# A tile of its own for every group of images, and all loads ahead of all stores on SP's ring, in a 180-degree rotation

## The chip, the cores and the metric

The kernel runs on one core of one Trainium2 chip; the other seven are idle. The metric is the device time of one execution in microseconds (us), as the median of several executions. A difference below 2% counts as "same", so nearly everything below is about why something large did not happen, and about effects of tenths of a per cent.

## The reference

```python
x = randn(32, 3, 256, 256).astype(float32)        # 25.17 MB
out = np.rot90(x, k=2, axes=(-2, -1))             # every 256x256 image turned by 180 degrees
```

Turning by 180 degrees is reversing the 65536 elements of each of the 96 images. There is no arithmetic: 25.17 MB come in, 25.17 MB go out.

## The kernel before: the parts that matter

The images are handled in three groups of 32. A group is a tile of 128 partitions by 16384 elements: four partitions for each image. The store's access pattern reverses the four quarters (`::-1`), VectorE reverses the elements within a partition.

```python
x4 = x.rearrange("b c h w -> (b c) (h w)").rearrange("(g n) (s e) -> g (n s) e", n=32, s=4)
o4 = out.rearrange("b c h w -> (b c) (h w)").rearrange("(g n) (s e) -> g n s e", n=32, s=4)
A  = pool.tile([P, E], ...)    # E = 16384: 64 KB a partition; Bt and Ct are the same
T  = pool.tile([P, J], ...)    # J = E // 8 = 2048

def load(t, g, lo=0, hi=E):
    nc.sync.dma_start(out=t[:, lo:hi], in_=x4[g][:, lo:hi])
def store(t, g):
    nc.sync.dma_start(out=o4[g][:, ::-1, :], in_=t[:, :])
# copy is a VectorE copy; back(t, lo, hi) is t[:, lo:hi] read backwards
def across(dst, src):                      # out of one tile into another: 4 copies
    for c in range(0, E, K):               # K = E // 4 = 4096
        copy(dst[:, c:c + K], back(src, E - c - K, E - c))
def inside(t):                             # in place, by way of T: 12 copies
    for lo in range(0, E // 2, J):
        hi = E - lo - J
        copy(T[:, :], back(t, hi, hi + J))
        copy(t[:, hi:hi + J], back(t, lo, lo + J))
        copy(t[:, lo:lo + J], T[:, :])

load(A, 0, 0, N); load(A, 0, N, E)         # N = 512
load(Bt, 1)
across(Ct, A);  store(Ct, 0)
load(A, 2)                                 # has to wait until A has been read out
inside(Bt);     store(Bt, 1)
across(Ct, A);  store(Ct, 2)
```

Below, "load 0" and "store 0" are those of group 0, and so on. Every DMA is issued from SP (the sync engine, which does nothing else here), so all of them are in one ring: the queue of one issuing engine, which the 16 DMA engines worked off in order. A "packet" is the piece that the profile records for one DMA engine, and a transfer "lands" when its last one is reported complete. ACT, below, is ScalarE, which issues into a ring of its own.

Of the kernel before, what the change touches and what calls it, by code (L numbers as in the profile page):

```python
# [2 lines left out]

os.environ.setdefault("NEURON_RT_ULTRASERVER_MODE", "4")

# [4 lines left out]


@with_exitstack
def kernel(
    ctx: ExitStack,
    tc: tile.TileContext,
    x: bass.AP,
    out: bass.AP,
):









    nc = tc.nc
    P = 128  # L30

    B, C, H, W = x.shape
    L = H * W
    G = 32
    E = L // 4
    K = E // 4
    J = E // 8
    N = E // 32

    x4 = x.rearrange("b c h w -> (b c) (h w)").rearrange(  # L40
        "(g n) (s e) -> g (n s) e", n=G, s=4)
    o4 = out.rearrange("b c h w -> (b c) (h w)").rearrange(
        "(g n) (s e) -> g n s e", n=G, s=4)

    pool = ctx.enter_context(tc.tile_pool(name="slots", bufs=1))
    A = pool.tile([P, E], x.dtype, tag="A")
    Bt = pool.tile([P, E], x.dtype, tag="B")
    Ct = pool.tile([P, E], x.dtype, tag="C")
    T = pool.tile([P, J], x.dtype, tag="T")

    def back(t, lo, hi):
        return t[:, hi - 1:(lo - 1 if lo else None):-1]

    def copy(dst, src):
        tc.keep_in_program_order(nc.vector.tensor_copy(out=dst, in_=src))  # L55

    def load(t, g, lo=0, hi=E):
        nc.sync.dma_start(out=t[:, lo:hi], in_=x4[g][:, lo:hi])  # L58

    def store(t, g):  # L60
        nc.sync.dma_start(out=o4[g][:, ::-1, :], in_=t[:, :])  # L61

    def across(dst, src):
        for c in range(0, E, K):
            copy(dst[:, c:c + K], back(src, E - c - K, E - c))

    def inside(t):
        for lo in range(0, E // 2, J):
            hi = E - lo - J
# [4 lines that stand above are left out]
    load(A, 0, 0, N)  # L74
    load(A, 0, N, E)
    load(Bt, 1)
    across(Ct, A)
    store(Ct, 0)
    load(A, 2)
    inside(Bt)  # L80
    store(Bt, 1)
    across(Ct, A)
    store(Ct, 2)


# [1 line left out]
_INS = ['x']  # L87
_OUTS = [((32, 3, 256, 256), 'float32')]


# [23 lines left out]
```

## Time and profile before

| | before |
|---|---|
| time, median of 3 | 123.36 us |
| span in the profile | 121.2 us |
| moved | 50.33 MB, mean 415 GB/s |
| share of the 16 DMA engines' span filled by packets | 97.4% |
| VectorE busy | 32.5 us, 20 copies |

A share of 97.4% says that the DMA engines are the bound. One more view, of SP's own waits, tells who holds back the issue of a transfer. Columns: who waited, for what, us in total, times, longest.

```profile
SPq L61 <- DVE Ct L55: 61.5, 2, 32.0
SPq L61 <- DVE Bt L55: 15.1, 1, 15.1
SPq L61 <- DMA Bt<-in_x_dram: 10.2, 1, 10.2
```

SP waits for VectorE in 76.6 of the 121.2 us (61.5 + 15.1).

### The profile page before, as it was taken

What the parts mean: (1) busy time and instruction counts of PE and PEld (TensorE: products, weight loads), DVE (VectorE), ACT (ScalarE), POOL (GpSimd) and SP (SyncE); (2) the same over time, 40 slices, a digit from 0 to 9 for tenths busy, and PEclk for the clock granted to TensorE, in tenths of its full rate; (3) what the DMA queues carried; (4) which work ended last, traced back from release to release, by engine and by line L of the source; (5) the groups of instructions that cost most, each with busy time, mean ns of one, the idle gap of its engine ahead of it and who ended that gap; (6) DMA issues with size and microseconds to landing.
All of it is one profiled execution on the core that took longest, in us unless ns stands there. A gap on an engine that the chain in (4) does not pass through costs nothing.

```text
span 121.2 us, 75 instructions
## 1 busy us (share of the span) xinstructions
DVE 32.5 (27%) x20; POOL 0.2 (0%) x4
## 2 busy tenths in 40 slices
DVE  0000000599400079999100000009990000000000
POOL 0000000000000000000000000000000000000000
DMA  9977987997899497799789977997798779877980
GB/s 336 421 335 335 650 356 335 433 606 346 346 454 584 173 519 346 346 519 519 346 346 627 411 346 346 649 389 346 346 649 389 346 346 649 389 346 346 649 389 0
DMA packets 1008, 50.33 MB, mean 415 GB/s; under 512 B 112, under 2 KB 112, under 8 KB 240
## 3 DMA queue, kind: packets, MB, share of 16 engines
q1 hardware_dynamic: 1008, 50.33, 97.4%
HBM read 25.17 MB, written 25.17 MB: 415 GB/s over the span
## 4 chain that ended last, share of the span: by engine, by line
DMA 58%; DVE 13%; DVEq 2%; SPq 1%; issue 0%
DMA A<-in_x_dram 58%; DVE Ct L55 13%; DVEq L109 2%; SPq L61 1%; SPq L58 0%; DVEq L55 0%
## 5 line engine op out<-in xcount | busy, mean ns | idle before, releaser
L55 DVE COPY Ct<-A 128x4096 f32<-128x4096 f32 x8 | 17.8, 2290 | 46.3 <-DMA A<-in_x_dram 46.3
L55 DVE COPY T<-Bt 128x2048 f32<-128x2048 f32 x4 | 4.9, 1227 | 11.6 <-DMA Bt<-in_x_dram 11.5
L55 DVE COPY Bt<-T 128x2048 f32<-128x2048 f32 x4 | 4.9, 1227 | 0.1
L55 DVE COPY Bt<-Bt 128x2048 f32<-128x2048 f32 x4 | 4.9, 1226 | 0.1
L98 POOL MEMSET const-bfloat16-1.0<- 128x1 bf16 x1 | 0.1, 102 | 0.0
L98 POOL MEMSET const-uint8-127<- 128x1 uint8 x1 | 0.1, 102 | 0.0
L98 POOL MEMSET const-float32-1.0<- 128x1 f32 x1 | 0.1, 99 | 0.0
L98 POOL MEMSET const-float32-0.0<- 128x1 f32 x1 | 0.1, 98 | 0.2 <-issue 0.2
## 6 DMA issues: line engine op xcount, KB each, us to landing
A<-in_x_dram SPq DMA_DIRECT2D x1, 7936.0 KB, 21.4
A<-in_x_dram SPq DMA_DIRECT2D x1, 256.0 KB, 2.8
out_dram<-Ct SPq DMA_DIRECT2D x2, 30.4
Bt<-in_x_dram SPq DMA_DIRECT2D x1, 41.4
A<-in_x_dram SPq DMA_DIRECT2D x1, 49.4
out_dram<-Bt SPq DMA_DIRECT2D x1, 43.0
```

Source lines behind the costliest of these rows:

```text
L55: tc.keep_in_program_order(nc.vector.tensor_copy(out=dst, in_=src))
L61: nc.sync.dma_start(out=o4[g][:, ::-1, :], in_=t[:, :])
L98: nc = _bacc.Bacc("TRN2", target_bir_lowering=False, num_devices=1)
L109: with _tile.TileContext(nc) as tc:
```

## The change

The third group gets the tile Ct for itself, so load 2 need not wait for A; each group is turned in place. With that, SP can issue all loads at the start.

```diff
-    K = E // 4
...
-    def across(dst, src):
-        for c in range(0, E, K):
-            copy(dst[:, c:c + K], back(src, E - c - K, E - c))
...
     load(A, 0, 0, N)
     load(A, 0, N, E)
     load(Bt, 1)
-    across(Ct, A)
-    store(Ct, 0)
-    load(A, 2)
-    inside(Bt)
-    store(Bt, 1)
-    across(Ct, A)
-    store(Ct, 2)
+    load(Ct, 2)
+    for g, t in enumerate((A, Bt, Ct)):
+        inside(t)
+        store(t, g)
```

The intent: the third load is no longer tied to the first group's turn, and SP's waits shrink to one a store. It is paid with copies: 36 in place of 20.

## The prediction

> **What bounds the kernel now.** I first read the page's table of 40 slices, its queue line and its row of DMA totals, to see whether any engine is busy without a pause. The first digit string is VectorE, the DMA row is the mean busy share of the core's 16 DMA engines.
>
> ```profile
> DVE  0000000599400079999100000009990000000000
> DMA  9977987997899497799789977997798779877980
> DMA packets 1008, 50.33 MB, mean 415 GB/s; under 512 B 112, under 2 KB 112, under 8 KB 240
> q1 hardware_dynamic: 1008, 50.33, 97.4%
> ```
>
> VectorE works in three islands (32.5 us of the 121.2 us span) with long rests. The DMA row has no rest: packets of the one queue fill 97.4% of the span on all 16 engines. 50.33 MB is twice the 25.17 MB of the input, so each byte goes in once and out once; there is no traffic to save. What is left of the span, 2.6% of 121.2 = 3.1 us, is the start before the first packet and the end after the last.
>
> Second, the chain of work that ended last, because at first sight it tells another story:
>
> ```profile
> 22.63 8.91 DVE Ct L55 x4
> 31.54 0.02 issue
> 31.56 0.63 SPq L61
> ...
> 32.31 49.42 DMA A<-in_x_dram
> 81.73 0.03 issue
> ```
>
> The third group's load is issued only at 32.3, after the first group was turned out of A, and takes 49.4 us to land. It looks as if a load issued 30 us earlier would bring the end forward. But only the last 19.3 us of those 49.4 are its own bytes; before them the ring still had the second load and the first store to carry. This chain follows semaphores and does not see the order within a ring.
>
> Third, a table by stage that I cut at the landings (22.6, 43.0 and 81.7 are in the chain and the timeline; the last store was issued at 90.76 and landed 29.6 later, at 120.4; 62.3 and 101.0 are the ends of the two stores between, which I placed a group's time later). Columns: stretch and its length, VectorE busy, POOL busy, TensorE clock, DMA share, GB/s.
>
> ```profile
> 0.00:22.60 22.60, 0.00 (x0) 0.20 (x4) 1.00 0.99 418
> 22.60:43.00 20.40, 8.90 (x4) 0.00 (x0) 1.00 1.01 411
> 43.00:62.30 19.30, 14.72 (x12) 0.00 (x0) 1.00 1.00 435
> 62.30:81.80 19.50, 0.00 (x0) 0.00 (x0) 1.00 0.99 430
> 81.80:101.00 19.20, 8.90 (x4) 0.00 (x0) 1.00 1.01 437
> ```
>
> In order these are load 0, load 1, store 0, load 2, store 1; the rest is store 2. A load and a store of 8.39 MB take the same time: from 43.0 to 120.4 go three stores and one load in 77.4 us, 19.35 us each, or 434 GB/s. Only load 1 is longer: 20.4 us, 1.05 us over. Two windows inside it show where; here "share" counts a packet whole in the window in which it starts:
>
> ```profile
> 38.00:40.00 2.00, 0.00 (x0) 0.00 (x0) 1.00 1.78 524
> 40.00:42.00 2.00, 0.00 (x0) 0.00 (x0) 1.00 0.00 0
> ```
>
> The last packet of load 1 on each engine starts near 39 and lasts much longer than its neighbours, and nothing starts until 42. It is the last packet ahead of the first store of the program. The second change from a load to a store, at 81.8, shows no such pause. VectorE is idle at 39, so it isn't the cause. I call this the **pause**; its cause isn't known from this trace.
>
> **What the Trainium skill says.** (1) "DMA: Bandwidth & Descriptors", section "Queues, rings and completion order": on each DMA engine the descriptors of one ring are consumed in ring order. The trace agrees: loads and stores follow each other whole, in issue order. So putting load 2 ahead of store 0 swaps two 19.35 us blocks, and can't overlap them. (2) The same page, section "Measured (HBM→SBUF, 128 partitions, SWDGE, issued from GpSimd)": a 16 MB load reached 425 GB/s, 97% efficiency. That is another issuing path; here the steady rate is 434 and the mean 415, so the kernel is already at the top of what either shows. (3) "VectorE: DVE Perf Modes", section "The perf-mode tier table (the rule you actually need)": an fp32 copy of 2048 elements in SBUF takes 1227 ns. The trace has 1227 and 1226 for the copies inside Bt, though they read backwards. (4) "SBUF — State Buffer", section "SBUF: two separate sides": a DMA issued from SP runs at full speed alongside a VectorE copy. The trace agrees: 435 GB/s in the stretch with 14.72 us of copies against 430 in the one with none.
>
> **The change part by part.**
>
> Copies. Groups 0 and 2 lose four copies of 128x4096 out of A into Ct, and gain twelve of 128x2048 in place.
>
> ```profile
> L55 DVE COPY Ct<-A 128x4096 f32<-128x4096 f32 x8 | 17.8, 2290 | 46.3 <-DMA A<-in_x_dram 46.3
> L55 DVE COPY T<-Bt 128x2048 f32<-128x2048 f32 x4 | 4.9, 1227 | 11.6 <-DMA Bt<-in_x_dram 11.5
> ```
>
> A group turned across lasted 22.63 to 31.54, 8.9 us. A group turned inside lasted 43.01 to 58.12 in the timeline, 15.1 us: twelve steps of 1227 ns and about 33 ns of semaphore between. So each of the two groups costs 15.1 - 8.9 = 6.2 us more, 12.4 in all, and VectorE's busy time becomes 36 x 1.227 = 44.2 us. On the path: none, if each store is ready before the ring reaches it (below).
>
> Loads. Load 2 needs no free buffer any more: its wait for the turn of group 0 (issue at 32.3) goes, and it is issued as SP's fourth instruction, near 2.1 us (1.63 plus the 0.43 us of the third). No bytes are saved. The ring's order becomes load 0, 1, 2, store 0, 1, 2 instead of load, load, store, load, store, store.
>
> The schedule, by 19.35 us a block: load 0 lands at 22.6 as now; load 1 at 41.95; load 2 at 61.3. With the pause in front of the first store (now in load 2) 62.35. Store 0 can be issued at 22.6 + 15.2 = 37.8, 24 us before the ring reaches it. Store 1: 41.95 + 15.2 = 57.2, needed at 81.7. Store 2: 62.4 + 15.2 = 77.6, needed at 101.05. Every store is queued over 20 us early, so the ring never runs dry. Landings of the stores: 81.7, 101.05, 120.4, and 0.8 us to the end: 121.2, the span of now. Sum of the change: +0 of bytes, +0 of 12.4 us of copies (all beside transfers), 0 for the pause if it moves with the first store, -1.05 if it does not come.
>
> **The rivals.**
> (a) *The early load shortens the path.* If the chain is taken at its word, load 2 lands at 62 instead of 82, and the end comes 19 us earlier, near 104. For it: the 49.4 us in the chain and 23.7 us of VectorE idle on that load. Against it: 50.33 MB at 434 GB/s are 116 us whatever the order, and store 0 is pushed back by what load 2 gains.
> (b) *VectorE's slower turning becomes a wait.* At worst 12.4 us of copies come onto the path, about 136. Against it: slacks of over 20 us at all three stores.
> (c) *Long runs of one direction run at another rate than the mix.* The kernel now already has two loads in a row and, at the end, two stores in a row, with the same 19.3 to 19.4 us as blocks that follow the other direction. A change of 1% in rate would be 1.2 us. A fourth load in the queue while the first still runs could hold up SP, but only its first store waits behind, with 24 us to spare.
> (d) *The pause.* It stays if it belongs to the first store (123.4), goes if it belonged to something particular to that moment (122.3), and could come again or grow at the only turn of direction left (124.4).
>
> **Range and chances.** I keep 0.7 on the pause staying and 0.3 on its going: 123.36 - 0.3 x 1.05 = 123.05; rounded towards no change, 123.2. The range is one pause either way: 122.2 to 124.2. The limits of 2% are 120.9 and 125.8: faster would need 2.5 us out of the 3.1 us that the ring is not filled, or a higher rate, 1%; slower would need a mechanism that the trace doesn't show, 2%; within 2%, 97%.
>
> **What would show each step.** In the changed kernel's profile: the DMA share stays at 97 to 98% with 50.33 MB; VectorE shows 36 copies of about 1227 ns, 44.2 us; SP issues four loads in the first 2.6 us and the stores near 37.8, 57.2 (58.2 with the pause in load 1) and 77.6; landings of loads at 22.6, 42 and 61.3 to 62.4; stores take about 43 us from issue to landing, because they queue; each 8.39 MB block takes 19.35 us; the pause, if there, sits just before the first store, near 58 to 62. I would be wrong if the DMA row showed a hole between the third load and the first store, if copies slowed down beside loads, or if blocks of one direction took clearly other than 19.35 us.

## The result and the profile after

The changed kernel ran at 122.91 us (median of 4), the kernel before at 123.28 in the same rounds. The ratio is 0.9968 with a 95% interval of 0.9951 to 0.9985: "same" at 2%. Ratios here are the mean time of one kernel's runs over that of the other's of the same rounds, so they aren't quite the ratio of the medians quoted. Executions over 1.5% slower than the fastest of the same kernel are left out of the means.

First the page of the changed kernel, the same rows as before: VectorE and DMA busy in tenths by slices of 3 us, and the queue's packets, MB and share.

```profile
DVE  0000000599994199998039999600000000000000
DMA  9977987897799879978989977997799779977980
q1 hardware_dynamic: 1008, 50.33, 97.4%
```

Two of VectorE's three islands have grown (the one in the middle had twelve copies before), and the last ends at 77.6 us instead of 90.7; the DMA row looks as it did and its share is the same to a tenth of a per cent. Then the table by stage, cut at this kernel's landings (stretch and length, VectorE busy, POOL busy, clock, DMA share, GB/s):

```profile
22.60:42.00 19.40, 14.72 (x12) 0.00 (x0) 1.00 1.00 432
42.00:62.40 20.40, 14.72 (x12) 0.00 (x0) 1.00 1.00 411
62.40:81.70 19.30, 14.72 (x12) 0.00 (x0) 1.00 1.00 435
81.70:101.00 19.30, 0.00 (x0) 0.00 (x0) 1.00 1.00 435
```

Now these are load 1, load 2, store 0, store 1. Each block of 8.39 MB takes 19.3 to 19.4 us, whatever the VectorE column says beside it. The one long block of 20.4 us, which was load 1 before, is now load 2: the pause has moved to stay ahead of the first store. Two short windows show it, as before at 38 to 42:

```profile
58.00:60.00 2.00, 0.00 (x0) 0.00 (x0) 1.00 1.78 524
60.00:62.00 2.00, 0.00 (x0) 0.00 (x0) 1.00 1.14 492
```

The share of 1.78 is that of packets which start near 58.5 and are counted whole there. By the packets' times none starts from 58.5 to 61.5; those in the second window are store 0's first. And the issues (size in KB where it is not the whole group, us from issue to landing):

```profile
Ct<-in_x_dram SPq DMA_DIRECT2D x1, 60.3
out_dram<-A SPq DMA_DIRECT2D x1, 43.9
out_dram<-Bt SPq DMA_DIRECT2D x1, 43.8
out_dram<-Ct SPq DMA_DIRECT2D x1, 42.7
```

Load 2 lands at 62.4 instead of 81.7, 19.3 us earlier. In return, store 0 takes 43.9 us from issue to landing, where in the kernel before it took some 30: it queues behind load 2. The two cancel, because they swapped places in one ring.

**How the pause is measured below.** The trace has a duration for every packet. A group's transfer has eight packets of 64 KB on each of 16 engines; each takes 2.418 us as a rule, 19.34 us for eight. The pause is the sum of a transfer's packet durations divided by 16, minus 19.34. For the kernel before it is 1.16 us at load 1 and 0.04 at load 2; for the changed kernel 1.14 at load 2.

### The profile page after: what moved, and what is told of

Its sections match the earlier page's. It is cut to its first block, busy times and chain, and to the rows that moved or that the text cites. A ratio compares the mean times of both kernels' runs of the same rounds, so it can differ in the third digit from the quotient of the medians.

```text
span 121.1 us, 94 instructions
## 1 busy us (share of the span) xinstructions
DVE 44.2 (36%) x36; POOL 0.2 (0%) x4
## 4 chain that ended last, share of the span: by engine, by line
DMA 33%; DVE 25%; another core or an unknown queue 4%; issue 1%; SPq 1%; DVEq 0%
DMA Bt<-in_x_dram 33%; DVE T L53 8%; DVE Ct L53 8%; DVE Bt L53 8%; SPq L56 1%; DVEq L53 0%
## 5 line engine op out<-in xcount | busy, mean ns | idle before, releaser
L53 DVE COPY T<-A 128x2048 f32<-128x2048 f32 x4 | 4.9, 1227 | 22.7 <-DMA A<-in_x_dram 22.6
L53 DVE COPY T<-Ct 128x2048 f32<-128x2048 f32 x4 | 4.9, 1227 | 5.4 <-DMA Ct<-in_x_dram 5.3
L53 DVE COPY T<-Bt 128x2048 f32<-128x2048 f32 x4 | 4.9, 1227 | 4.4 <-DMA Bt<-in_x_dram 4.3
L53 DVE COPY Bt<-T 128x2048 f32<-128x2048 f32 x4 | 4.9, 1227 | 0.1
L53 DVE COPY A<-T 128x2048 f32<-128x2048 f32 x4 | 4.9, 1227 | 0.1
L53 DVE COPY Ct<-Ct 128x2048 f32<-128x2048 f32 x4 | 4.9, 1227 | 0.1
L53 DVE COPY Bt<-Bt 128x2048 f32<-128x2048 f32 x4 | 4.9, 1227 | 0.1
L53 DVE COPY A<-A 128x2048 f32<-128x2048 f32 x4 | 4.9, 1227 | 0.1
L53 DVE COPY Ct<-T 128x2048 f32<-128x2048 f32 x4 | 4.9, 1227 | 0.1
## 6 DMA issues: line engine op xcount, KB each, us to landing
out_dram<-A SPq DMA_DIRECT2D x1, 43.9
```

Source lines behind the costliest of these rows:

```text
L53: tc.keep_in_program_order(nc.vector.tensor_copy(out=dst, in_=src))
```

## The experiments

Twelve kernels ran, all with right results. The theory is that of the prediction: the ring is never empty, so neither the order in it nor the copies count, and a store only has to be queued before the ring gets to it. Each experiment starts from the changed kernel.

### 1. The tiles and the copies, with the old order (a "column" is a group's tile)

```diff
     load(Bt, 1)
-    load(Ct, 2)
-    for g, t in enumerate((A, Bt, Ct)):
-        inside(t)
-        store(t, g)
+    inside(A);  store(A, 0)
+    load(Ct, 2)
+    inside(Bt); store(Bt, 1)
+    inside(Ct); store(Ct, 2)
```

> One part alone: every group has its own column and is turned inside it, but SP issues load, load, store 0, load 2, store 1, store 2 as in the kernel before. Theory (the ring is never empty, order and copies cost nothing): 122.9 to 123.4 us, the 1.05 us pause back at the end of load 1 (near 39 to 43 us), load 1 landing at 43.0. If the 0.3% that the change gained belongs to the order of the ring, this kernel is as slow as the one before (ratio 1.000, 123.3 us); if it belongs to the copies, ratio 0.997. Rival (third load is late, so its early issue is what counts): no, since load 2 lands at 81.7 here and the time would have to differ.

It ran at 122.86 us, the kernel before at 122.98 in the same rounds, ratio 0.9985 (0.9969 to 1.0001). Load 2 was issued at 38.3 instead of 2.1 us and landed 20 us later than in the changed kernel, and the time is the same. So the early load is worth nothing, as the ring argument says. Its pause was back at load 1, 0.77 us. The run doesn't settle to which part a gain of 0.3% would belong; its interval has both 0.997 and 1.000.

### 2 and 3. How late may a store be issued?

Here extra copies, whose result is overwritten, make VectorE slower by a known amount: 8 more for each group in one kernel, 12 more in the other.

```diff
     for g, t in enumerate((A, Bt, Ct)):
+        for i in range(8):                  # 12 in the second kernel
+            copy(T[:, :], back(t, 0, J))
         inside(t)
```

> The changed kernel with eight more copies of 128x2048 into T for each group (20 in all per group, result still right). Theory (copies are hidden while each store is issued before the ring reaches it): 20 x 1.26 = 25.2 us a group, stores issued at 47.9, 73.1 and 98.3, needed at 62.4, 81.8 and 101.1, so no change: 122.9 us, DMA share still 97%. Rival (more VectorE work beside transfers slows them or comes onto the path): plus up to 30 us.

> Twelve more copies for each group (24 per group). Theory: 30.3 us a group, stores issued at 52.9, 83.2 and 113.5; the second is 1.4 us and the third some 10 us behind what the ring needs, so the end is 113.5 + 1.4 until the first packet + 19.35 + 0.8 = 135 us of span, 136.9 us of time, and the DMA row gets a hole ahead of store 2. Rival (VectorE's copies never reach the path): 122.9.

With 8 more the time was 123.33 us against 123.11 for the kernel before (ratio 1.0017, 0.9989 to 1.0044): same, though VectorE's busy time rose from the changed kernel's 44.2 us to 73.6. With 12 more it was 137.11 us (ratio 1.1135, 1.1106 to 1.1164); 136.9 had been worked out. SP's issues in these two kernels (start, duration, transfer), the first three lines from the one with 8 more:

```profile
47.78 0.63 SPq L59 DMA_DIRECT2D out_dram<-A  x1
73.01 0.55 SPq L59 DMA_DIRECT2D out_dram<-Bt  x1
98.23 0.54 SPq L59 DMA_DIRECT2D out_dram<-Ct  x1
```

```profile
83.24 0.54 SPq L59 DMA_DIRECT2D out_dram<-Bt  x1
113.51 0.54 SPq L59 DMA_DIRECT2D out_dram<-Ct  x1
```

In the first kernel store 2 goes into the ring at 98.2, some 3 us before store 1 ends at 101: nothing is lost. In the second it goes in at 113.5, when store 1 has been over for some 9 us. Store 1 was late there too: it goes in at 83.2, and store 0's last packet had ended at 81.3. The DMA row of that page has the large hole:

```profile
DMA  9699697978979789799889777779790007779790
```

One slice there is 3.4 us. The three zeros are the ring running dry; the row counts a packet whole where it starts, and by the packets' own times nothing runs from 104.0 to 114.7. The engines stand empty for 3.5 us ahead of store 1 and 10.9 ahead of store 2, which is the loss of 14. This is the threshold to which the prediction's slack of over 20 us refers: 41 us more of copies in all (73.6 less 32.5 of the kernel before) cost nothing, 56 us more cost 14 us.

### 4 and 5. What is the pause? A small store early

A piece of 128x512 of group 0 is turned as soon as it is there and stored ahead of the rest, in one kernel from SP behind load 0, in the other from ACT's ring.

```diff
     load(A, 0, N, E)
+    copy(S[:, :], back(A, 0, N))
+    nc.sync.dma_start(out=o4[0][:, ::-1, E - N:], in_=S[:, :])   # nc.scalar in the second kernel
     load(Bt, 1)
     ...                                                          # store 0 leaves these columns out
```

> The changed kernel with a 128x512 piece of group 0 turned first and stored from SP ahead of load 1; its packets come on the ring right behind load 0. Theory 1 (the pause belongs to the first store of the program): the last packet of load 0 takes 3.3 to 3.9 us instead of 2.34, the last packet of load 2 is back at 2.42, time about the changed kernel's plus up to 0.5 us for eight small packets per engine, 122.9 to 123.4. Theory 2 (the pause belongs to a change from a long run of loads to stores): it stays at load 2, near 59 to 62 us, and perhaps comes at load 0 also: 122.9 to 124.5.

> As the run before, with the small early store issued from ACT's ring instead of SP's, near 5 us, while SP's ring carries load 0. Theory 1a (first store, and it holds the whole DMA engine): a pause of about 1.1 us near 5 to 8 us on each engine, none at load 2; time as the changed kernel's, 122.9 to 123.4. Theory 1b (first store, but it holds only its own ring): SP's packets go on meanwhile and the ring ends about 1.1 us earlier: 121.8 to 122.3 us, faster than both kernels by near 1%. Theory 2 (change of direction after loads): pause stays near 59 to 62 us, time 122.9 to 123.5.

From SP: 122.66 us, ratio to the kernel before 0.9978 (0.9962 to 0.9994). The packets ahead of the small store took 2.62 us (median of 16 engines) in place of 2.34, and the pause at load 2 was 0.42 us instead of 1.14. From ACT: 122.90 us, ratio 0.9993 (0.998 to 1.0006), pause at load 2 of 0.95 us; the eight small packets on each engine slipped in between SP's at 0.08 us each, and no pause came with them. The run from ACT came out as theory 2 had it; the one from SP lies outside both, so neither theory holds as I wrote it. Had the pause belonged to the first store of the program, it would have gone from load 2; had it belonged to the change from a run of loads alone, it should not have shrunk to 0.42. Each of these pauses is read from one trace, and the changed kernel alone shows 1.14 in one trace and 0.97 in another, so sizes closer than that tell nothing.

### 6. Load 0 in one piece

```diff
-    load(A, 0, 0, N)
-    load(A, 0, N, E)
+    load(A, 0)
```

> The changed kernel with load 0 as one transfer in place of a 128x512 one and the rest, which the new order of copies no longer uses (its first copy reads the end of A). Theory (the time is the packets on the ring plus a fixed start and end): eight small packets per engine go, whose part of the ring was about 1 us for 0.26 MB against 0.6 us at the steady rate, so 0.3 to 0.5 us less, 122.4 to 122.6 us. Rival (the small transfer fills the start-up latency for nothing): same time, 122.9.

A miss: 122.91 us, ratio 0.9997 (0.9985 to 1.0009), no gain. The small transfer of 0.26 MB seems to fill a start in which the ring would not have run at its full rate. Load 0's packets took 19.95 us an engine in one piece and 19.98 in two, and VectorE's first copy, which waits for load 0, began at 22.64 us here and at 22.63 with the two.

### 7. All stores from ACT's ring

```diff
     def store(t, g):
-        nc.sync.dma_start(out=o4[g][:, ::-1, :], in_=t[:, :])
+        nc.scalar.dma_start(out=o4[g][:, ::-1, :], in_=t[:, :])
```

> The changed kernel with all stores issued from ACT's ring, so that store 0 need not wait behind load 2 and can share the engines with it. Theory (bytes at the engines' rate bind, whatever order or mix): 122.9 us within 0.5%, or about 1 us less if the first store's pause holds only its own ring and the loads go on; load 2 lands later (up to 81 us), store 0 earlier. Rival (reads and writes mixed move at another rate): a difference of more than 1% either way in the stretch from 38 to 62 us and in the time.

131.82 us, ratio 1.0744 (1.0681 to 1.0807; a fourth run of 133.22 was set aside as slow). This is the largest effect that a change of order or ring had. The theory failed, and the rival in the expectation came true. The stretch in which load 2 and store 0 share the engines, with the stretch ahead of it:

```profile
22.60:42.00 19.40, 14.72 (x12) 0.00 (x0) 1.00 1.03 432
42.00:82.00 40.00, 14.72 (x12) 0.00 (x0) 1.00 0.98 369
```

The engines are as busy (share 0.98) and move 15% less: on each engine the packets of load 2 and store 0 took turns, and load 2's took 2.94 us in the median and up to 4.2, store 0's 2.43, where those of one ring take 2.42. Both transfers landed near 89.6, so 16.78 MB took 47.7 us from load 1's landing, where the changed kernel needs 39.7 (42.0 to 81.7). The profiled run lost 7.9 us (129.0 against 121.1 us of span), and the packets tell of what: 4.8 us are longer packets (122.7 us an engine in place of 117.9), 1.1 us are a hole near 105 (load 2 landed late, so store 2 was issued only at 104.8), and most of the rest is the end, where the engines finished up to 2.4 us apart.

### 8. Store 0 and load 2 in halves that alternate, on one ring

```diff
-    load(Ct, 2)
-    for g, t in enumerate((A, Bt, Ct)):
-        inside(t)
-        store(t, g)
+    inside(A);  part(A, 0, 0, E // 2)        # part: store of some columns
+    load(Ct, 2, 0, E // 2)
+    part(A, 0, E // 2, E)
+    load(Ct, 2, E // 2, E)
+    inside(Bt); store(Bt, 1)
+    inside(Ct); store(Ct, 2)
```

> The order of the kernel before, each tile its own, but store 0 and load 2 in halves that alternate: load 0, load 1, half of store 0, half of load 2, half of store 0, half of load 2, store 1, store 2: three turns from loads to stores. If every turn costs a pause of about 1 us: 2 us more, 125. If only the first (theory 1) or only a turn after a long run of loads (theory 2): one pause of 0.8 to 1.15 at load 1, none at the halves, 122.9 to 123.3.

122.87 us, ratio 0.9975 (0.9953 to 0.9997; one run of 125.5 set aside as slow). The pause was 0.67 us at load 1 and under 0.02 at both later turns from a load to a store. So changing direction on one ring cost nothing as such here, three turns no more than one.

### 9. A second run of two loads, late

The diff is against the kernel of experiment 1.

```diff
     inside(A);  store(A, 0)
     load(Ct, 2)
+    load(A, 0)                               # again, unused
     inside(Bt); store(Bt, 1)
```

> Old order with a load more: load 0, load 1, store 0, load 2, load 0 again (unused, into A), store 1, store 2. A second run of two loads stands ahead of the second turn to a store. Time 123 + 19.35 = 142.3 us. Theory 2 (run of loads): the second turn, near 101 us, has a pause of 0.7 to 1.15 us like the first, where the kernel before had 0.04 after a single load. Theory 1 (first store of the program): 0.1 us or less there.

142.48 us in a single run; 142.3 had been worked out from the 19.35 us of a block. The trace of it has the pause twice, at load 1 and at the load added (stretches as above):

```profile
22.60:42.70 20.10, 14.63 (x12) 0.00 (x0) 1.00 1.00 417
62.10:81.40 19.30, 0.00 (x0) 0.00 (x0) 1.00 1.00 435
81.40:101.20 19.80, 14.72 (x12) 0.00 (x0) 1.00 1.00 424
```

By packets 0.79 us at the first and 0.41 at the second, which is between what the two theories said (0.7 to 1.15, and 0.1 or less). A turn after a single load had 0.04 (before) and 0.07 (experiment 1). So a later store can have a pause too, after two loads more than after one, and the first has more.

### 10. Two early pieces

Pieces of groups 0 and 1 stored from SP between the loads, each as in experiment 4 (the diff is shortened: stores 0 and 1 leave their pieces out).

```diff
     load(A, 0, 0, N); load(A, 0, N, E)
+    piece(S, A, 0)
-    load(Bt, 1)
+    load(Bt, 1, 0, N); load(Bt, 1, N, E)
+    piece(S2, Bt, 1)
     load(Ct, 2)
```

> Small pieces of groups 0 and 1 are turned first and stored from SP between load 0 and load 1, and between load 1 and load 2. In the run with one early store the last packets ahead of a store were 0.28 us longer at load 0 and 0.42 at load 2, against 1.14 in one place in the changed kernel. Theory 2 (the pause grows with the run of loads since the last store in the ring): each of three turns has 0.3 us or less, 122.3 to 122.7 us, faster than both kernels by 0.2 to 0.5%. Theory 1 (first store only, the rest spread by chance): load 2's last packet stays at 0.4 us over, 122.6 to 122.8.

122.68 us, ratio 0.9989 (0.9959 to 1.0019). The pause at load 2 stayed at 0.42 us, as theory 1 had it; the last packets of load 0 took 2.67 us in place of 2.34, those of load 1 no longer than usual. A small store between does not end a run of loads: theory 2 fails in this form, and theory 1 doesn't explain experiment 9.

### 11. The changed kernel once more, as a control

> The changed kernel again, on the chip of the runs beside it, as the control for the sizes below 1%: on one chip the kernel before ran at 122.98 us, not 123.28, and kernels that differ from the changed one by nothing that matters ran at 122.9. If the 0.3% gain is real on every chip: ratio 0.997. If it lies between the chips' and runs' own spread: 0.999 to 1.000. Pause of 1.1 us ahead of store 0.

122.85 us against 123.00 for the kernel before in the same rounds, ratio 0.9982 (0.9966 to 0.9999), between the two readings. The pause was 0.97 us. So a gain of 0.3% and of 0.2% came in two sets of rounds; but the kernel of experiment 6, which does the same work as the changed one, shows none (0.9997), and the kernel before itself ran at 122.98 to 123.28 in different sets. Whether a gain of that size belongs to the change is not shown.

### 12. Two rings, both with loads

```diff
-    load(Bt, 1)
+    nc.scalar.dma_start(out=Bt[:, :], in_=x4[1][:, :])
```

> The changed kernel with load 1 issued from ACT's ring, so that loads 0 and 1 share the DMA engines from the start, packet by packet; all stores stay on SP. It tells apart why stores from ACT's ring cost 7%. If two rings that alternate cost something by themselves, whatever the direction: about 7.7 us for 16.8 MB shared there, so 130 us here as well. If it is loads and stores alternating that costs: both loads land near 42 us, store 0 is issued near 57 and store 1 near 72, both before the ring reaches them (62 and 82), 122.9 us within 0.5%.

122.46 us, ratio to the kernel before 0.9954 (0.9929 to 0.9979). The first stretch here has both loads:

```profile
0.00:42.00 42.00, 0.00 (x0) 0.20 (x4) 1.00 1.00 424
42.00:62.00 20.00, 19.11 (x16) 0.00 (x0) 1.00 0.98 419
```

The run doesn't tell what it was made for, because the two loads did not share the engines as the expectation has it. Both were to land near 42 us; their issues say otherwise (KB where it is not the whole group, us from issue to landing):

```profile
A<-in_x_dram SPq DMA_DIRECT2D x1, 7936.0 KB, 41.2
Bt<-in_x_dram ACTq DMA_DIRECT2D x1, 25.2
```

Load 1, issued at 0.7 us, landed near 26, and the large part of load 0, issued at 1.2, near 42. On each engine the eight packets of 64 KB of load 1 took turns with the eight of 2 KB that make up load 0's small first piece. Then load 1 was through (its packets ran from 2.0 to 23.2 us), and load 0's large packets followed alone (22.2 to 41.9). So large packets of two rings never took turns here, and an obvious rival for experiment 7 stays untested: that two rings with large packets cost something whatever the direction. Shown is that 7% come with large load and large store packets taking turns from two rings; that the direction is the cause is not shown. Small packets of another ring cost next to nothing between large ones, whether loads (here, with 2.42 us as the median of load 1's packets) or stores (experiment 5). This kernel with load 0 in one piece, as in experiment 6, would be the test.

Store 0 is issued at 57.5, only a few us before the ring needs it, and it is enough. This kernel has the smallest pause at the first store, 0.20 us, and is the fastest that I ran: 0.3% below the control, which ran on the same chip but in another set of rounds. I wouldn't call that more than a hint.

## Why the prediction was right, point by point

**Bound and path.** "Every store is queued over 20 us early, so the ring never runs dry": right. The stores were issued at 37.76, 57.18 and 77.59 us; 37.8, 57.2 and 77.6 had been worked out. Experiments 2 and 3 show that this slack is what hides the copies, and where it ends.

**Copies.** VectorE shows 36 copies of 1227 ns, 44.2 us, as predicted, and none of the 11.7 us more is on the path. Rival (b), that slower turning becomes a wait, was rightly ruled out; experiment 3 shows what it would have taken.

**The early load.** Rival (a), 19 us from load 2's earlier landing, was wrong for the reason given. The landing did come 19.3 us earlier (81.7 to 62.4), and store 0 was pushed back by as much. Experiment 1, with the load issued 36 us later, has the same time.

**One direction or mixed.** Rival (c) was rightly ruled out for one ring: blocks stay at 19.3 to 19.4 us, and in experiment 8 halves that alternate are no slower. For the kernel with the stores on another ring it would not have been (experiment 7: 7% slower); whether the direction or the second ring costs that is open.

**The pause.** It was given 0.7 to stay and 0.3 to go. It stayed and moved with the first store, at the place named ("near 58 to 62"). Its cause is open. The traces, one for each kernel, speak against three readings: that it belongs to the first store alone (0.41 us at a later turn in experiment 9), to every turn (0.02 in experiment 8), or to the run of loads since the last store, be that store ever so small (0.42 in both 4 and 10). It differs between runs of one design: 1.14 and 0.97 us for the changed kernel in two traces.

**The size.** 123.2 had been predicted and 122.91 came, well within 122.2 to 124.2. That the point lies 0.16 us below the 123.36 of no change, and so nearer to the result, is luck: that discount was for a pause that goes, and the pause stayed. The changed kernel was faster by 0.2 to 0.3% in its two sets of rounds, which no step of mine explains: the two profiled executions differ by only 0.1 us of span and 0.06 us of time (122.95 and 122.89), so most of it lies in executions of the kernel before that have no trace. The step "+0 of bytes, +0 of copies, 0 for the pause" holds to that size and no further.

## What to carry to other kernels

When one ring fills 97% of the span, count its bytes and its order before you believe the chain of waits: a load that "takes 49 us" may, as here, be 30 us of queueing, and issuing it earlier only moves the queue to someone else. Ask of each transfer not how long its issuer waits but whether it is issued before the ring runs dry; up to that point slower copies are free, and beyond it they cost in full. When the DMA engines are the bound, try large loads and stores in one ring first: here they ran at 435 GB/s in order, and at 369 where they took turns from two rings.

## What the Trainium skill lacked or had wrong

- "DMA: Bandwidth & Descriptors", section "Issuing engines are not separate DMA queues": it says that issuing from several engines only saves the sequencer's time. Here, moving the stores from SP to ACT cost 7.4% (131.82 against 123.11 us), with 369 GB/s in the stretch where large load and store packets alternate against 432 to 435 in one ring. With loads on both rings there was no loss (122.46 us), but there large packets of the two never alternated. The page has no word on a loss where two rings interleave.
- The same page, section "Measured (HBM→SBUF, 128 partitions, SWDGE, issued from GpSimd)": it has loads from GpSimd only, up to 425 GB/s; the load streams from SP elsewhere on the page are of 1 MiB a DMA, and no page that I consulted has a rate for stores from SBUF on this chip. Here loads and stores of 8.39 MB issued from SP both ran at 434 to 435 GB/s, 2.418 us for a packet of 64 KB on one engine.
- No page that I consulted has the pause ahead of a first large store behind loads: 0.67 to 1.16 us with everything on one ring and no store before it, 0.42 with a small store ahead, 0.41 at a later turn behind two loads, under 0.1 behind one.
